# U's first half in a decoder layer: matmuls of 512 columns instead of 256, and an addition of two sums

## The chip, the core and the metric

The kernel runs on one core of one Trainium2 chip. Five engines with queues of their own work on one on-chip memory: TensorE (PE) multiplies matrices into the eight PSUM banks, VectorE (DVE) and ScalarE (ACT) do element-wise work and read PSUM, GpSimd (POOL) does very little here, and SyncE (SP) issues the transfers from HBM. The metric is the device time of one execution, in microseconds (us). Every engine takes its instructions in the order of its queue; where an instruction needs a result of another engine it waits for a semaphore, and all that is queued behind it on its engine waits too.

## The reference

One decoder layer on 256 tokens of 1024 channels. First a mixer (a state-space model and attention, side by side), a residual and a LayerNorm; then PEER, a retrieval over 128 x 128 single-neuron experts, a residual and a second LayerNorm. The change lies in PEER:

```python
q = (xc @ w_q).astype(jnp.float32).reshape(TOKEN_CHUNK, PEER_HEADS, 2, PEER_HALF)
s = jnp.einsum('thcd,hcnd->thcn', q, sub_keys.astype(jnp.float32))
s1, i1 = lax.top_k(s[:, :, 0], PEER_TOPK)
s2, i2 = lax.top_k(s[:, :, 1], PEER_TOPK)
...
top, pos = lax.top_k(cand, PEER_TOPK)
eidx = jnp.take_along_axis(cidx, pos, axis=-1)
g = jax.nn.softmax(top, axis=-1)
u = expert_u[eidx].astype(jnp.float32)
act = jax.nn.gelu(jnp.einsum('td,thkd->thk', xc.astype(jnp.float32), u))
out = jnp.einsum('thk,thkd->td', g * act, expert_v[eidx].astype(jnp.float32))
```

## The kernel before

It gathers no experts. It computes the activation of all 16384 experts for all 256 tokens (x times U), multiplies by gates that are zero for experts not chosen, and multiplies by V. U and V come in 128 tiles each, a tile being 128 experts x 1024 channels in fp32, 512 KB.

*Precision.* A product in full precision is made of three in a faster type (fp32r): each operand is split into an upper half (a rounded copy, `hi`) and a lower half (the rest, `lo`), and hi x hi, hi x lo and lo x hi are summed in PSUM; lo x lo is left out. For U's first half `split3` does this with the weights: ACT casts `hi` (L78), DVE subtracts for `lo` (L79). The transfer's buffer `raw` has four copies, `hi` and `lo` three each. The normed activations stand in x's halves `xh` and `xl`, split once.

*U, a tile.* `dense` (L1122 on) makes 24 matmuls at L1129: for each of 8 slices of 128 channels a weight block of 128x128 is loaded into the array, and 256 columns (the tokens) of x run past it. The order is hi with xh, hi with xl, lo with xh, eight each, all into one sum of 128 experts x 256 tokens.

*U, first half.* Tiles 0 to 63, two at a time in `u_pair` (L854 to L860): both sums lie in one bank of the pool `psb` (two banks), and one ACT instruction takes the gelu from PSUM into the store `act` (L859). Beside it runs the routing, on DVE mostly (`route`: top-16 searches L812 to L816, index arithmetic L879 to L917; `weigh`: the softmax and two groups of transposes on PE, L935). The routing is cut into 44 steps which are handed out over the first 26 pairs, behind each pair's last subtraction. Its index copies `fv` (L908) are on ACT.

*U, second half.* Tiles 64 to 127, again through `dense`; beside them the gates are made (PE L1004, ACT L998, DVE L993 to L995 and L1011), in the pool `pw` (four banks).

*V.* For each tile of V PE makes 12 matmuls of 512 columns (L1056), with blocks of the activations as the weights in the array and the V tile running past.

The order on each engine follows from a scheduler that goes by priorities and data; it is fixed when the kernel is built. In the mixer, two stretches of memory that later hold `xh` and `xl` (tags `xh`, `xl`) hold the transposed input `xT` and a tile of attention weights; at the very end they hold two V tiles.

Of the kernel before, what the change touches and what calls it, by code (L numbers as in the profile page):

```python
# [8 lines left out]
F32 = mybir.dt.float32  # L9
F32R = mybir.dt.float32r  # L10
# [5 lines left out]
OP = mybir.AluOpType  # L16
# [3 lines left out]
D = 1024  # L20
T = 256
ND = D // 128
# [31 lines left out]
def layer(ctx, tc, I, out, tap=None, upto=None):  # L54
    nc = tc.nc
    V, S, P, PE = nc.vector, nc.scalar, nc.gpsimd, nc.tensor

    const = ctx.enter_context(tc.tile_pool(name="const", bufs=1))
# [3 lines left out]
    def load(src):  # L62
        raw = stream.tile([128, 1024], F32, tag="raw", bufs=RAWB, name="raw")
        nc.sync.dma_start(raw, src.rearrange("p a b -> p (a b)") if len(src.shape) == 3 else src)
        return raw

    def split(raw, eng=V, hi=None, lo=None):
        if hi is None:
            hi = stream.tile([128, 1024], F32R, tag="hi", bufs=HIB, name="hi")
            lo = stream.tile([128, 1024], F32R, tag="lo", bufs=LOB, name="lo")  # L70
        S.copy(hi, raw)  # L71
        eng.tensor_tensor(lo, raw, f32(hi), op=OP.subtract)  # L72
        return hi, lo

    def split3(raw):
        hi, lo = (stream.tile([128, 1024], F32R, tag=t, bufs=n, name=t)
                  for t, n in (("hi", HIB), ("lo", LOB)))
        S.copy(hi, raw)  # L78
        return hi, lo, V.tensor_tensor(lo, raw, f32(hi), op=OP.subtract)  # L79
# [20 lines left out]
    def pbank(shape):  # L100
        return ps.tile(shape, F32, tag="w", bufs=4, name="pw")

    def sbank(shape):
        return ps.tile(shape, F32, tag="s", bufs=2, name="psb")

    def abank(shape):
        return ps.tile(shape, F32, tag="a", bufs=2, name="pa")
# [3 lines left out]
    with ExitStack() as px:  # L111
# [6 lines left out]
        with ExitStack() as mx:  # L118
            sb = mx.enter_context(tc.tile_pool(name="sb", bufs=1))
# [5 lines left out]
                return P if CFG[g][i] == "P" else V  # L125

            prm = se.tile([128, 1088], F32, name="prm")
            xT = const.tile([128, ND, T], F32, tag="xh", name="xT")
            nc.sync.dma_start(prm[:, 0:48], I["prm"][:, 0:48])


# [357 lines left out]
            def masks():  # L489
# [5 lines left out]
                for j in range(4):  # L495
# [6 lines left out]
            rs = sb.tile([128, 2, 8], F32, name="rs")  # L502

            pTs = [sb.tile([128, 4, 2, 128], F32, name="pT0"),
                   const.tile([128, 4, 2, T], F32, tag="xl", name="pT1")]

            def attend(b):

# [148 lines left out]
            for k in (4, 5, 6, 7):  # L657
                if k in LATE:
                    r = W3[:, 2 * (k - 6):2 * (k - 6) + 2]
# [7 lines left out]
            for k, t in enumerate(("Kin", "qk")):  # L667
                r = sb.tile([128, 2, 1024], F32R, tag=t, name="W0")
# [8 lines left out]
            ng = sb.tile([128, D], F32, tag="Rt", name="ng")  # L677
            S.activation(ng, g1[:, 0], AF.Copy, scale=-1.0)
            h1b = sb.tile([128, 2, D], F32, tag="rot", name="h1b")
            xh = const.tile([128, ND, T], F32R, tag="xh", name="xh")  # L680
            xl = const.tile([128, ND, T], F32R, tag="xl", name="xl")

            st = {}

# [41 lines left out]
            for q in range(4):  # L726
# [6 lines left out]
                if q < 2:  # L733
                    r = late.tile([128, 2, 1024], F32R, tag="W4", bufs=2, name="W4")
                    hi, lo = r[:, 0], r[:, 1]
                else:
                    hi, lo = (stream.tile([128, 1024], F32R, tag=t, bufs=n, name=t)
                              for t, n in (("hi", HIB), ("lo", LOB)))
# [57 lines left out]
    act = [None, None]  # L796
# [7 lines left out]
    with ExitStack() as rx:  # L804
        sb = rx.enter_context(tc.tile_pool(name="rt", bufs=1))
# [23 lines left out]
        for hc in range(4, 16):  # L829
            raw = load(I["w_q"][hc])  # L830
            if hc == 4:
                with tc.issue_after(w4dma.ins):
                    nc.sync.dma_start(keys, I["keys"])
            hi, lo = (stream.tile([128, 1024], F32R, tag=t, bufs=n, name=t)
                      for t, n in (("hi", HIB), ("lo", LOB)))
# [4 lines left out]
            pt = abank([128, 2, T])[:, 0]  # L840
# [11 lines left out]
            tap("sco", sco)  # L852

        def u_pair(i):  # L854
            pt = sbank([128, 2, T])
            for r in range(2):
                hi, lo, low = split3(load(I["u"][i + r]))
                dense(PE, pt[:, r], hi, lo, xh, xl)
            return low, S.activation(act[0][:, i // 2].rearrange("p t r -> p r t"), pt,  # L859
                                     AF.Gelu_apprx_tanh)  # L860

        gn = sb.tile([128, 2, 128], F32, name="gn")
# [90 lines left out]
        for n in range(HALF // 2):  # L953
            low, ac = u_pair(2 * n)
            with tc.issue_after(low.ins), tc.issue_after(ac.ins) if n >= PAIRS else ExitStack():
                while done < min(STEPS, -(-STEPS * (n + 1) // PAIRS)):
                    done += 1
                    next(steps, None)
                if n == PAIRS - 1:
                    assert next(steps, 0) == 0  # L960
                if n >= PAIRS + GAP - 1:
                    next(last, None)
# [6 lines left out]
    def v_split(half, i, own=None):  # L969
        hi, lo, wh, wl = own or (None, None) + tuple(  # L970
            wk.tile([128, T], F32R, tag=t, bufs=2, name=t) for t in ("wh", "wl"))
        hi, lo = split(load(I["v"][half * HALF + i]), V, hi, lo)
        S.copy(wh, of_tile(half, i))  # L973
        V.tensor_sub(wl, of_tile(half, i), f32(wh))  # L974
        return hi, lo, wh, wl
# [4 lines left out]
    with tc.tile_pool(name="gk", bufs=1) as gk:  # L980
# [41 lines left out]
        for n in range(HALF // 2):  # L1022
# [5 lines left out]
            pt = sbank([128, 2, T])  # L1028
            for r in range(2):
                hi, lo = split(load(I["u"][HALF + 2 * n + r]))  # L1030
# [28 lines left out]
    def v_tile(half, i, t=None):  # L1059
        t = t or v_split(half, i)  # L1060
        for b in range(2):
            v_mm(b, t, half == 0 and i == 0, False)
# [13 lines left out]
    LAST = 4  # L1076
    for i in range(HALF - LAST):
        v_tile(1, i)
    xs = [const.tile([128, 2, 1024], F32R, tag=t, name="vx") for t in ("xh", "xl")]
    last = [v_split(1, HALF - LAST + i, None if i < 2 else  # L1080
                    (xs[0][:, i - 2], xs[1][:, i - 2]) + tuple(
                        wk.tile([128, T], F32R, tag=t, bufs=2, name="wx") for t in ("wx", "wy")))
            for i in range(LAST)]
    st = {}
# [37 lines left out]
def dense(PE, pt, hi, lo, xh, xl, last=None, beside=None):  # L1122

    order = [(hi, xh), (hi, xl), (lo, xh)]
    if last is xl:
        order = [(hi, xh), (lo, xh), (hi, xl)]
    for n, (w, x) in enumerate(order):
        for d in range(ND):
            PE.matmul(pt, w[:, 128 * d:128 * d + 128], x[:, d], start=n == 0 and d == 0,  # L1129
                      stop=n == 2 and d == ND - 1)  # L1130
        if beside is not None and n == 1:
            next(beside, None)
# [76 lines left out]
```

## Time and profile before

| | |
|---|---|
| median of 3 runs | 978.0 us (975.91 to 979.0) |
| the profiled execution | 976.38 us, its span 974.6 us |
| granted TensorE clock, mean | 0.988 |
| PE busy | 953.0 us, 98% |
| DVE busy | 683.7 us, 70% |
| ACT busy | 527.6 us, 54% |
| L1129 (U) and L1056 (V) in the chain that ended last | 38% and 35% |

The page sums busy time over stages with different limits; what the change is worth is read from U's first half alone, which runs from 210 to 396 us. A matmul's record is longer than the distance to the next one, since matmuls are pipelined, so PE's pace is read from the starts in the timeline.

### The profile page before, as it was taken

What the parts mean: (1) busy time and instruction counts of PE and PEld (TensorE: products, weight loads), DVE (VectorE), ACT (ScalarE), POOL (GpSimd) and SP (SyncE); (2) the same over time, 40 slices, a digit from 0 to 9 for tenths busy, and PEclk for the clock granted to TensorE, in tenths of its full rate; (3) what the DMA queues carried; (4) which work ended last, traced back from release to release, by engine and by line L of the source; (5) the groups of instructions that cost most, each with busy time, mean ns of one, the idle gap of its engine ahead of it and who ended that gap; (6) DMA issues with size and microseconds to landing.
All of it is one profiled execution on the core that took longest, in us unless ns stands there. A gap on an engine that the chain in (4) does not pass through costs nothing.

```text
span 974.6 us, 16536 instructions
## 1 busy us (share of the span) xinstructions
PE 953.0 (98%) x6286; PEld 851.0 (87%) x6286; DVE 683.7 (70%) x1431; ACT 527.6 (54%) x995; POOL 21.4 (2%) x25
## 2 busy tenths in 40 slices
PE   7999999999999999999999999999999999999995
PEld 3876977999999999999999999888888888888884
DVE  8974477997777664978889887555555555555556
ACT  3214454555445446888778776455555555555552
POOL 3000002000000000000000000000000000000002
PEclk9996999999999999999999999999999999999998
DMA  8320283356565555455545455556666676666661
GB/s 331 124 66 23 70 274 114 127 186 198 180 187 182 181 187 179 147 156 167 155 140 165 152 153 160 174 192 194 191 196 194 193 278 193 195 194 195 195 194 44
DMA packets 49791, 166.25 MB, mean 171 GB/s; under 512 B 5296, under 2 KB 9392, under 8 KB 49584
## 3 DMA queue, kind: packets, MB, share of 16 engines
q1 hardware_dynamic: 49712, 165.20, 53.6%
q8 instruction: 49, 0.80, 0.3%
q14 instruction: 30, 0.25, 0.1%
HBM read 163.09 MB, written 2.10 MB: 169 GB/s over the span
## 4 chain that ended last, share of the span: by engine, by line
PE 93%; DVE 4%; DMA 1%; ACT 1%; issue 0%; SPq 0%; DVEq 0%; ACTq 0%
PE psb L1129 38%; PE pw L1056 35%; PE pw L1004 3%; PE pw L174 3%; PE pa L1129 2%; PE pw L653 2%; PE psb L163 2%; PE pw L519 1%; PE pa L163 1%; DMA w<-in_w_in 1%; PE pw L394 1%; PE psb L448 1%; PE pa L754 1%; PE pw L544 1%; DMA tail<-in_ln_g 1%; PE pa L533 0%
## 5 line engine op out<-in xcount | busy, mean ns | idle before, releaser
L72 DVE TENSOR_TENSOR lo<-raw,hi 128x1024 fp32r<-128x1024 f32 x195 | 238.6, 1224 | 156.4 <-ACT hi L71 152.3
L71 ACT CAST hi<-raw 128x1024 fp32r<-128x1024 f32 x195 | 205.0, 1051 | 217.2 <-PE pw L1056 162.7
L1056 PE MATMUL pw<-hi,wh 128*128 128x512 f32 x492 | 152.0, 390 | 1.0 <-ACT wh L973 1.0
L1056 PE MATMUL pw<-hi,wl 128*128 128x512 f32 x492 | 152.3, 390 | 0.2
L1056 PE MATMUL pw<-lo,wh 128*128 128x512 f32 x492 | 151.9, 390 | 0.0
L1129 PE MATMUL psb<-xh,lo 128*128 128x256 f32 x1024 | 148.5, 288 | 0.0
L1129 PE MATMUL psb<-xh,hi 128*128 128x256 f32 x1024 | 144.5, 284 | 0.4 <-ACT act L859 0.4
L1129 PE MATMUL psb<-xl,hi 128*128 128x256 f32 x1024 | 143.6, 283 | 0.0
L1129 PEld LDWEIGHTS psb<-xh,hi 128*128 128x128 f32 x1024 | 132.1, 192 | 0.8 <-ACT act L859 0.8
L1129 PEld LDWEIGHTS psb<-xl,hi 128*128 128x128 f32 x1024 | 132.1, 192 | 0.0
L1129 PEld LDWEIGHTS psb<-xh,lo 128*128 128x128 f32 x1024 | 131.2, 192 | 0.0
L78 ACT CAST hi<-raw 128x1024 fp32r<-128x1024 f32 x64 | 67.0, 1047 | 87.4 <-PE psb L1129 78.2
L79 DVE TENSOR_TENSOR lo<-raw,hi 128x1024 fp32r<-128x1024 f32 x64 | 78.1, 1220 | 51.3 <-ACT hi L78 51.1
L1056 PEld LDWEIGHTS pw<-hi,wh 128*128 128x128 f32 x492 | 92.3, 188 | 20.4 <-ACT wh L973 1.4
L1056 PEld LDWEIGHTS pw<-hi,wl 128*128 128x128 f32 x492 | 92.3, 188 | 20.1 <-DVE wl L974 1.1
L1056 PEld LDWEIGHTS pw<-lo,wh 128*128 128x128 f32 x492 | 92.4, 188 | 19.1
L998 ACT ACTIVATE o<-eq,gL 128x128 f16<-128x128 f16 x256 | 85.1, 440 | 0.6 <-DVE eq L994 0.6
L1011 DVE TENSOR_TENSOR act<-pw,act 128x256 f32<-128x256 f32 x124 | 38.3, 351 | 26.6 <-PE pw L1004 26.4
L973 ACT CAST wh<-act 128x256 fp32r<-128x256 f32 x123 | 51.3, 418 | 0.8 <-PE pw L1056 0.8
L974 DVE TENSOR_TENSOR wl<-act,wh 128x256 fp32r<-128x256 f32 x123 | 51.3, 418 | 0.0
L1004 PE MATMUL pw<-o,o 128*128 128x128 f16 x512 | 40.3, 220 | 0.0
L1004 PEld LDWEIGHTS <-o 128*128 128x128 f16 x512 | 29.5, 97 | 2.6
(307 smaller groups left out, 977.4 us busy)
## 6 DMA issues: line engine op xcount, KB each, us to landing
raw<-in_u SPq DMA_DIRECT2D x128, 512.0 KB, 3.5
raw<-in_v SPq DMA_DIRECT2D x128, 512.0 KB, 3.6
w<-in_w_in SPq DMA_DIRECT2D x15, 512.0 KB, 8.5
raw<-in_w_q SPq DMA_DIRECT2D x12, 512.0 KB, 3.8
raw<-in_w_out SPq DMA_DIRECT2D x8, 512.0 KB, 3.9
raw<-in_w_q SPq DMA_DIRECT2D x8, 256.0 KB, 3.9
xT<-in_xT SPq DMA_DIRECT2D x4, 256.0 KB, 5.1
raw<-in_w_glu SPq DMA_DIRECT2D x2, 512.0 KB, 3.7
```

The lines of the kernel that those rows point to most:

```text
L71: S.copy(hi, raw)
L72: eng.tensor_tensor(lo, raw, f32(hi), op=OP.subtract)
L78: S.copy(hi, raw)
L79: return hi, lo, V.tensor_tensor(lo, raw, f32(hi), op=OP.subtract)
L163: PE.matmul(pt[b], xT[:, d, 128 * b:128 * b + 128], w[:, 512 * k:512 * k + 512], start=d == 0, stop=d == 7)
L973: S.copy(wh, of_tile(half, i))
L974: V.tensor_sub(wl, of_tile(half, i), f32(wh))
L998: S.activation(o2[:, 1, i // 2, :, i % 2], eq[:, i // 2, :, i % 2], AF.Copy, scale=gL[:, t0 + i:t0 + i + 1])
L1004: PE.matmul(pt[:, i], o1[:, (q + i) // 2, :, i % 2], o2[:, k, (q + i) // 2, :, i % 2], start=k == 0, stop=k == 1)
L1011: V.tensor_tensor(a, gp[:, :, HALF // 2 * h:HALF // 2 * h + n], a, op=OP.mult)
L1056: PE.matmul(acc[b][c], x[:, tk], w[:, 512 * c:512 * c + 512], start=first and j == 0, stop=last and j == 2)
L1129: PE.matmul(pt, w[:, 128 * d:128 * d + 128], x[:, d], start=n == 0 and d == 0, stop=n == 2 and d == ND - 1)
```

## The change

In U's first half the upper weights meet both halves of x in one matmul of 512 columns. For that `xh` and `xl` become one tile `x2`, in which the 256 columns of xh and the 256 of xl of a channel slice lie side by side. The sum over xh (with the lower weights' products) and the sum over xl now stand beside each other in one bank. ACT copies the second out of PSUM (`ul`), DVE adds it to the first (`us`), and the gelu reads `us`. The sums lie in the four-bank pool `pw` now. One upper slice is left to the end of the tile, behind the lower weights, since it closes the sum over both halves.

```diff
@@ layer: the tiles of x
-            xT = const.tile([128, ND, T], F32, tag="xh", name="xT")
+            x0 = const.tile([128, 2, ND * T], F32, tag="x2", name="x0")
+            xT = x0[:, 0].rearrange("p (d t) -> p d t", t=T)
...
-                   const.tile([128, 4, 2, T], F32, tag="xl", name="pT1")]
+                   x0[:, 1].rearrange("p (n i t) -> p n i t", n=4, i=2)]
...
-            xh = const.tile([128, ND, T], F32R, tag="xh", name="xh")
-            xl = const.tile([128, ND, T], F32R, tag="xl", name="xl")
+            x2 = const.tile([128, ND, 2, T], F32R, tag="x2", name="x2")
+            xh, xl = x2[:, :, 0], x2[:, :, 1]
...
         def u_pair(i):
-            pt = sbank([128, 2, T])
+            us = sb.tile([128, 2, T], F32, tag="us", bufs=2, name="us")
             for r in range(2):
                 hi, lo, low = split3(load(I["u"][i + r]))
-                dense(PE, pt[:, r], hi, lo, xh, xl)
-            return low, S.activation(act[0][:, i // 2].rearrange("p t r -> p r t"), pt,
+                pt = pbank([128, 2, T])
+                for d in range(ND - 1):
+                    PE.matmul(pt, hi[:, 128 * d:128 * d + 128], x2[:, d], start=d == 0, stop=False)
+                for d in range(ND):
+                    PE.matmul(pt[:, 0], lo[:, 128 * d:128 * d + 128], xh[:, d], start=False, stop=False)
+                PE.matmul(pt, hi[:, D - 128:], x2[:, ND - 1], start=False, stop=True)
+                ul = sb.tile([128, T], F32, tag="ul", bufs=2, name="ul")
+                S.copy(ul, pt[:, 1])
+                V.tensor_tensor(us[:, r], pt[:, 0], ul, op=OP.add)
+            return low, S.activation(act[0][:, i // 2].rearrange("p t r -> p r t"), us,
                                      AF.Gelu_apprx_tanh)
```

PE's queue, two tiles of U's first half, before (the tile `psb` is the sum, `hi` and `lo` the weights):

```order
L1129 MATMUL psb<-xh,hi 128x256 x8
L1129 MATMUL psb<-xl,hi 128x256 x8
L1129 MATMUL psb<-xh,lo 128x256 x8
L1129 MATMUL psb<-xh,hi 128x256 x8
L1129 MATMUL psb<-xl,hi 128x256 x8
L1129 MATMUL psb<-xh,lo 128x256 x8
```

and now, where `x_1087` is x2 and `pw` the sum:

```order
L864 MATMUL pw<-x_1087,hi 128x512 x7
L866 MATMUL pw<-x_1087,lo 128x256 x8
L867 MATMUL pw<-x_1087,hi 128x512
L864 MATMUL pw<-x_1087,hi 128x512 x7
L866 MATMUL pw<-x_1087,lo 128x256 x8
L867 MATMUL pw<-x_1087,hi 128x512
```

A tile has 16 matmuls instead of 24, and its last one uses the upper weights.

ACT's queue at the start of U's first half, before (from the score copies of the routing, `sco`, to the third gelu):

```order
L824 COPY sco<-pw 128x128 x5
L78 CAST hi<-raw 128x1024 x2
L859 ACTIVATE act_1317<-psb 128x2x256
L908 CAST fv<-topi 128x2048
L78 CAST hi<-raw 128x1024
L908 CAST fv<-topi 128x2048
L78 CAST hi<-raw 128x1024
L859 ACTIVATE act_1317<-psb 128x2x256
L78 CAST hi<-raw 128x1024 x2
L859 ACTIVATE act_1317<-psb 128x2x256
```

and now:

```order
L826 COPY sco<-pw 128x128 x5
L869 COPY ul<-pw 128x256
L78 CAST hi<-raw 128x1024
L869 COPY ul<-pw 128x256
L78 CAST hi<-raw 128x1024
L871 ACTIVATE act_1315<-us 128x2x256
L920 CAST fv<-topi 128x2048
L869 COPY ul<-pw 128x256
L78 CAST hi<-raw 128x1024
L920 CAST fv<-topi 128x2048
L869 COPY ul<-pw 128x256
L78 CAST hi<-raw 128x1024
```

Each cast `hi`, which is for the tile three ahead, stands behind a copy `ul`, and of the two `fv` one stands ahead of the copy for tile 2 and one ahead of that for tile 3.

DVE's queue, from the subtraction for tile 2 to behind that for tile 3, before:

```order
L79 TENSOR_TENSOR lo<-raw,hi 128x1024
L812 MAX tops<-sco 128x8
L813 MAX_INDEX topi<-tops,sco 128x8
L814 MATCH_REPLACE tmp<-tops,sco 128x128
L815 MAX tops<-tmp 128x8
L816 MAX_INDEX topi<-tops,tmp 128x8
L79 TENSOR_TENSOR lo<-raw,hi 128x1024
L812 MAX tops<-sco 128x8 x2
L813 MAX_INDEX topi<-tops,sco 128x8
```

and now:

```order
L79 TENSOR_TENSOR lo<-raw,hi 128x1024
L814 MAX tops<-sco 128x8
L815 MAX_INDEX topi<-tops,sco 128x8
L816 MATCH_REPLACE tmp<-tops,sco 128x128
L817 MAX tops<-tmp 128x8
L818 MAX_INDEX topi<-tops,tmp 128x8
L870 TENSOR_TENSOR us<-pw,ul 128x256
L79 TENSOR_TENSOR lo<-raw,hi 128x1024
L814 MAX tops<-sco 128x8 x2
L815 MAX_INDEX topi<-tops,sco 128x8
L816 MATCH_REPLACE tmp<-tops,sco 128x128
L870 TENSOR_TENSOR us<-pw,ul 128x256
```

The addition for a tile stands ahead of the subtraction for the tile three ahead; the routing's searches stand behind it.

## Rows read from the trace of the kernel before

**Rows 1.** The page: its head, its first part and its fourth part.

```profile
span 974.6 us, 16536 instructions
PE 953.0 (98%) x6286; PEld 851.0 (87%) x6286; DVE 683.7 (70%) x1431; ACT 527.6 (54%) x995; POOL 21.4 (2%) x25
...
PE 93%; DVE 4%; DMA 1%; ACT 1%; issue 0%; SPq 0%; DVEq 0%; ACTq 0%
PE psb L1129 38%; PE pw L1056 35%; PE pw L1004 3%; PE pw L174 3%; PE pa L1129 2%; PE pw L653 2%; PE psb L163 2%; PE pw L519 1%; PE pa L163 1%; DMA w<-in_w_in 1%; PE pw L394 1%; PE psb L448 1%; PE pa L754 1%; PE pw L544 1%; DMA tail<-in_ln_g 1%; PE pa L533 0%
```

**Rows 2.** The chain in order of time: start us, us, engine, tile, line, count.

```profile
210.96 177.49 PE psb L1129 x1479
388.48 1.05 ACT hi L71
389.53 0.55 ACT act L859
...
624.64 162.11 PE pw L1056 x714
```

**Rows 3.** Five stretches of the span; their columns stand in the first line.

```profile
core 0: us, PE busy (x) PEld busy (x) DVE busy (x) ACT busy (x) POOL busy (x), PEclk, DMA share, GB/s
211.00:349.24 138.24, 138.24 (x1154) 138.24 (x1153) 104.26 (x293) 70.18 (x78) 0.00 (x0) 1.00 0.61 187
349.24:388.48 39.24, 39.24 (x329) 39.24 (x328) 19.40 (x22) 20.35 (x23) 0.00 (x0) 1.00 0.60 188
624.60:786.80 162.20, 162.16 (x715) 134.42 (x716) 93.05 (x121) 80.97 (x118) 0.00 (x0) 1.00 0.61 192
211.00:222.52 11.52, 11.52 (x98) 11.52 (x97) 9.99 (x37) 6.71 (x8) 0.00 (x0) 1.00 0.70 213
222.52:234.04 11.52, 11.52 (x98) 11.52 (x97) 9.64 (x41) 7.02 (x9) 0.00 (x0) 1.00 0.64 204
```

**Rows 4.** Timeline of PE in U's first half: start us, us, engine, line, instruction.

```profile
299.96 1.12 PE L1129 MATMUL psb<-xh,hi 128*128 128x256 f32 x8
...
300.92 1.12 PE L1129 MATMUL psb<-xl,hi 128*128 128x256 f32 x8
...
301.88 1.12 PE L1129 MATMUL psb<-xh,lo 128*128 128x256 f32 x8
```

**Rows 5.** Timeline of PE in V.

```profile
703.20 0.62 PE L1056 MATMUL pw<-hi,wl 128*128 128x512 f32 x2
703.65 0.62 PE L1056 MATMUL pw<-lo,wh 128*128 128x512 f32 x2
704.11 0.62 PE L1056 MATMUL pw<-hi,wh 128*128 128x512 f32 x2
704.56 0.62 PE L1056 MATMUL pw<-hi,wl 128*128 128x512 f32 x2
```

**Rows 6.** Groups of the whole span by shape: count, busy us, mean ns, idle before.

```profile
L843 ACT COPY qT<-pa 128x256 f32<-128x256 f32 x12 | 4.5, 372 | 0.0
...
L1011 DVE TENSOR_TENSOR act<-pw,act 128x256 f32<-128x256 f32 x64 | 27.1, 424 | 26.6 <-PE pw L1004 26.4
...
L917 DVE TENSOR_TENSOR df<-best 128x128 f32<-128x128 f32 x2 | 0.6, 284 | 0.0
```

**Rows 7.** Groups of DVE and ACT from 211 to 388.5 us.

```profile
L79 DVE TENSOR_TENSOR lo<-raw,hi 128x1024 fp32r<-128x1024 f32 x63 | 76.9, 1220 | 51.3 <-ACT hi L78 51.1
...
L78 ACT CAST hi<-raw 128x1024 fp32r<-128x1024 f32 x61 | 63.8, 1046 | 83.6 <-PE psb L1129 78.2 <-DVE abf L896 2.5 <-DVE topi L816 1.8
L859 ACT ACTIVATE act<-psb 128x512 f32<-128x512 f32 x30 | 19.4, 648 | 0.0
```

**Rows 8.** Timeline of ACT at the start of U.

```profile
218.74 1.90 ACT L908 CAST fv<-topi 128x2048 bf16<-128x2048 uint32 x1 [1.45 <-DVE topi L816]
220.54 1.04 ACT L78 CAST hi<-raw 128x1024 fp32r<-128x1024 f32 x1
221.49 1.89 ACT L908 CAST fv<-topi 128x2048 bf16<-128x2048 uint32 x1
```

**Rows 9.** Timeline of PE at the start of U and at the seam.

```profile
209.99 0.36 PE L1129 MATMUL psb<-xh,hi 128*128 128x256 f32 x1
210.25 0.71 PE L823 MATMUL pw<-keys,qT 128*128 128x128 f32 x4
210.72 1.08 PE L1129 MATMUL psb<-xh,hi 128*128 128x256 f32 x7
...
389.46 0.27 PE L935 MATMUL psb<-ident,gn 128*128 128x128 f32 x1
390.12 1.10 PE L1129 MATMUL psb<-xh,hi 128*128 128x256 f32 x7 [0.39 <-ACT act L859]
```

More of the change, by code (lines that the diff above doesn't have):

```diff
@@ L1078, in layer @@
         v_tile(1, i)
-    xs = [const.tile([128, 2, 1024], F32R, tag=t, name="vx") for t in ("xh", "xl")]
+    xs = const.tile([128, 2, 2, 1024], F32R, tag="x2", name="vx")
     last = [v_split(1, HALF - LAST + i, None if i < 2 else
-                    (xs[0][:, i - 2], xs[1][:, i - 2]) + tuple(
+                    (xs[:, 0, i - 2], xs[:, 1, i - 2]) + tuple(
                         wk.tile([128, T], F32R, tag=t, bufs=2, name="wx") for t in ("wx", "wy")))
```

## The prediction

> **What bounds the kernel now.** I read the page first: its first part gives each engine's busy time, its fourth the chain of work that ended last [rows 1]. TensorE (PE) is busy 98% of the span and holds 93% of the chain; two lines carry three quarters of it, L1129 (the U products, 38%) and L1056 (the V products, 35%). The reader is to see that only PE's time counts, unless a change makes another engine late. The chain in order of time [rows 2] then says where PE runs without a pause: in the first half of U for 177.49 us (1479 matmuls in one piece), and in V for 162.11 us. Before the last two tiles of that half is one seam where ScalarE (ACT) is on the chain for 1.6 us. The stretches [rows 3] say the same: in U's first half PE is busy for all of 138.24 us, VectorE (DVE) 104.26 and ACT 70.18, and the granted clock is 1.00 there and in V, so both stretches are at the 2.4 GHz level and their rows may be compared.
>
> PE's busy time says nothing of its pace, since matmuls overlap. The pace is the distance between starts in the timeline. In U eight 256-column matmuls start every 0.96 us [rows 4], 120.0 ns each; 177.49 us over 1479 is the same. In V six 512-column matmuls take from 703.20 to 704.56 us [rows 5], 226.7 ns each (162.11 over 714 gives 227.0). Both have a 128x128 weight load of their own and the same operand type. Twice 120.0 is 240.0: a matmul of double width is 13.3 ns cheaper than two, so each has a fixed part of about 13 ns beside its columns. The whole change lives on that.
>
> **The change part by part.** (a) *Matmuls.* A tile of U had 24 matmuls of 256 columns, 24 x 0.1200 = 2.880 us. Now it has 8 of 512 (upper weights against both halves of x) and 8 of 256 (lower weights): 8 x 0.2267 + 8 x 0.1200 = 2.773 us. That is 0.107 us less in each of 64 tiles, 512 pairs merged: -6.8 us, all on the path. No column is saved. The bounds: if the fixed part goes wholly with the merged weight load, 13.3 ns a pair is what V's rows say; from 227.0 ns it is 13.0, 6.7 us. If a 512-column matmul in this place kept 240 ns, nothing is gained.
>
> The row shows about 13 ns of fixed cost per matmul at the 2.4 GHz level [rows 4, 5]. The Trainium skill (TensorE: Matmul & The Clock Gate, "Back-to-back issue gap") gives the isolated gap as columns over 2.4 plus about 2.5 ns. By it the merge would save 512 x 2.5 ns = 1.3 us, an estimate from that page, and the change would not be seen; the trace disagrees with its 109 ns at 256 columns by 11 ns and with its 216 ns at 512 by the same 11, so here the measurement decides.
>
> (b) *The two sums.* Each tile adds an ACT copy of 128x256 from PSUM and a DVE addition of 128x256 with one operand in PSUM. The copy has a row of exactly its shape, L843 at 372 ns. For the addition the nearest is L1011 at 424 ns (PSUM and SBUF in, strided out); from below, half the elements take 284 ns at L917 [rows 6]. I take 0.424. Over 64 tiles that is 23.8 us of ACT and 27.1 us of DVE. The gelu reads SBUF instead of PSUM; at 648 ns [rows 7] I leave it as it is.
>
> All of it lies beside PE if both engines keep up. ACT: 70.18 us in 48 tiles is 1.46 us a tile (138.24 / 2.880 = 48), 1.83 with the copy, of 2.773. DVE: 104.26 / 48 = 2.17, with the addition 2.60 of 2.773, 94%. In the first eight tiles DVE is denser: 9.99 + 9.64 us [rows 3] are 2.45 a tile, 2.88 with the addition, 0.10 more than PE takes, so it falls 0.8 us behind in eight tiles. From 349 us on (39.24 us, 19.40 of DVE) there is room.
>
> (c) *The wait.* The addition waits for the copy, which waits for the tile's last matmul; behind the addition DVE has the subtraction for the lower weights of the tile three ahead, and behind the copy ACT has that tile's cast (the order shows both). Let a tile end at E. Copy 0.37, cast 1.05, subtraction 1.22 [rows 6, 7] end at about E + 2.7. PE wants those lower weights two tiles and seven 512-column matmuls later, at E + 2 x 2.773 + 7 x 0.227 = E + 7.1. That is 4.4 us of cover. The upper weights are now read to the tile's end and so their buffer comes free a third of a tile later than before; this is inside the same E, since the cast stands behind the copy anyhow. In the trace the cast waits for PE (83.6 us of idle before it, 78.2 of them ended by PE), and the subtraction for the cast (51.1) [rows 7]: both run as soon as a buffer comes free and are far ahead of PE.
>
> The tightest place is where ACT makes two 1.9 us index copies (fv), at 218.74 and 221.49 us [rows 8]. They now stand ahead of the copies and casts of tiles 2 and 3 in ACT's queue. Tile 0 begins at 209.99 and four score matmuls cut in for 0.6 us [rows 9], so tile 6 starts at 210.6 + 6 x 2.773 = 227.2. The first fv waits for an index of DVE, which now has two additions (0.85 us) ahead of it: 219.6. From there ACT does fv, copy, cast, fv, copy, cast: 2 x (1.89 + 0.37 + 1.05) = 6.6 us, so tile 6's upper weights are there at 226.2: 1.0 us to spare. The second such place, near 291 us, is like it with a less loaded DVE. I put +0.3 us for stalls, from 0 to +2.
>
> (d) *PSUM.* The first half's sums leave the two-bank pool for the four-bank pool, so a late addition holds PE only after four tiles. At the seam the transposes of the routing results take one of the two banks, and PE waited for a gelu from 389.57 (389.46 and its 0.11) to 390.12 [rows 9]: 0.55 us that go. What is late there next is the gate products' ACT work, which now begins a little earlier; from 0 to -0.8, I take -0.5.
>
> (e) *Layout.* x's halves lie interleaved in one tile. No instruction outside U's first half changes place apart from the scheduling around the seam, and the second half reads 256 contiguous columns as before. The weights come at 187 GB/s in U's first half [rows 3]; 2.880 / 2.773 of that is 194, and V takes 192 without a pause of PE. Nothing, within +-0.5.
>
> Sum: -6.8 - 0.5 + 0.3 = -7.0 us. The profiled execution took 976.4 us (its span 974.6 and 1.8 around it), so 969.4. The median of the runs is 978.0, 1.6 above it, and the forecast for a median is 978.0 - 7.0 = 971.0.
>
> **The rivals.**
> 1. *DVE and ACT give part of it back.* For it: 94% load in 48 tiles, over 100% in eight, and the fv places. Against: 1.0 us and more of cover at the tightest. If tiles 5 to 8 stall 1 us each, and near 291 us again as much in half, 3 to 4 us return: 974.5.
> 2. *The double width costs 240 ns here*, or the fixed part is as small as a page has it. For it: the operand order differs from V's (weights stationary, x moving, an output that covers a bank of two halves). Against: the widths in [rows 4, 5] share the same surplus. Gain 0 to 1.3 us, with the seam 0.5: 977. The rule is that of the Trainium skill named in (a), as far as the traces bear it out.
> 3. *Slower: DVE becomes the bound by waiting at its addition.* DVE is in order; if it always reaches the addition before ACT's copy is done, it stands for the copy (0.37 and the hand-over, some 0.5 us) with the routing work queued behind, and a tile costs 2.17 + 0.42 + 0.50 = 3.09 us. Over 48 tiles that is 48 x (3.09 - 2.88) = +10.3, less 16 x 0.107 = 1.7 for the others: 978.0 + 8.6 = 986.6. It decides from a wait of 0.28 us a tile on. For it: the addition sits in the order close behind the previous subtraction. Against: a DVE that lags does not wait, one that waits has caught up, and 4.4 us of cover stand between it and PE; it takes a shorter cover than the buffers give.
>
> **How the numbers follow.** The forecast 0.71, rival 1 0.12, rival 2 0.09, rival 3 0.08. A measurement of this kernel can tell about 0.3%, 2.9 us, from no change. The forecast is faster, with little left over; rival 1 mostly (0.08 of 0.12); rival 2 is the same; rival 3 slower, or, where it is mild, the same (0.01). Faster 0.79, same 0.14, slower 0.07. The forecast's own range is -4.5 to -8.5: 969.5 to 973.5. The runs before spread from 975.9 to 979.0, so a median may lie 2 us off; the range takes rivals 1 and 2 in: 968 to 977.5.
>
> **What would show it.** In the profile after: starts of the 512-column matmuls 0.227 us apart, the 256-column ones 0.120, a tile every 2.77 us; U's first half without a pause and about 7 us shorter; DVE some 25 us busier and still waiting for the cast in most tiles from 349 us on; the copy near 0.37 and the addition near 0.42 us; no wait for a gelu at the seam. I am wrong if the starts lie 0.240 apart (rival 2), if the U lines have idle time ended by the cast or the subtraction in many tiles (rivals 1 and 3), or if time is lost in the second half or in V, where I count none.

## The result, and the profile after

The change makes the kernel 0.6% faster: 971.87 us against 978.1 us (medians of five runs each), a ratio of 0.9942 with a 95% interval of 0.9926 to 0.9957. The forecast was 971.0 us.

The profiled execution of the changed kernel took 973.51 us (span 971.7), only 2.9 us less than that of before. That is one execution against one, and its mixer ran at a lower granted clock. The same work up to the output projection's last piece, once at 0.94 and once at 0.91 of full clock (columns as in [rows 3]), before:

```profile
0.00:131.40 131.40, 124.02 (x653) 94.12 (x654) 95.82 (x259) 47.92 (x108) 8.68 (x17) 0.94 0.40 132
```

and after:

```profile
0.00:133.67 133.67, 126.11 (x653) 96.08 (x654) 97.08 (x260) 48.88 (x109) 8.68 (x17) 0.91 0.39 132
```

Each kernel's runs spread over some 4 us by that clock (with this change 969.22 us at a mean of 0.990, 973.51 at 0.984), so I compare stages within the traces, where U and V run at 1.00, beside the medians. The two ends of U are in the chain in order of time: the last piece of the routing's projection and V's first. Before:

```profile
206.47 2.87 PE pa L1129 x24
...
614.18 7.75 PE pw L1056 x34
```

and after:

```profile
208.74 2.87 PE pa L1141 x24
213.24 1.62 PE pw L864 x7
214.86 0.95 PE pw L866 x8
...
610.14 7.75 PE pw L1068 x34
```

From 206.47 to 614.18 are 407.71 us, from 208.74 to 610.14 are 401.40: U's whole stage is 6.3 us shorter, where I had 7.0. The one piece of 1479 matmuls of [rows 2] now shows as groups of 7, 8 and 1, since the width changes.

PE's pace in the timeline after, a tile and its neighbours, to be held against [rows 4] and [rows 5]:

```profile
302.24 0.40 PE L867 MATMUL pw<-x,hi 128*128 128x512 f32 x1
302.47 1.77 PE L864 MATMUL pw<-x,hi 128*128 128x512 f32 x7
304.08 1.12 PE L866 MATMUL pw<-x,lo 128*128 128x256 f32 x8
305.03 0.40 PE L867 MATMUL pw<-x,hi 128*128 128x512 f32 x1
305.27 0.62 PE L864 MATMUL pw<-x,hi 128*128 128x512 f32 x2
```

From 302.47 to 305.27 a tile takes 2.80 us; over many tiles of the chain it is 2.793 (213.24 to 383.64 us in 61 tiles). The eight 256-column matmuls start 0.119 us apart, (305.03 - 304.08) / 8. The eight 512-column ones take 304.08 - 302.24 = 1.84 us, 0.230 each, not 0.2267. Of the terms of (a) it is the one that came out another way.

The stretch with the routing, to be held against the first of [rows 3]:

```profile
212.99:351.00 138.01, 138.01 (x792) 121.41 (x791) 122.13 (x344) 85.89 (x128) 0.00 (x0) 1.00 0.61 191
```

PE is busy for the whole of it; DVE has gone from 104.26 to 122.13 us, ACT from 70.18 to 85.89, and neither holds PE. The groups after, from 212 to 394 us, which answer to [rows 6] and [rows 7]:

```profile
L79 DVE TENSOR_TENSOR lo<-raw,hi 128x1024 fp32r<-128x1024 f32 x64 | 78.0, 1219 | 15.2 <-ACT hi L78 14.5
...
L870 DVE TENSOR_TENSOR us<-pw,ul 128x256 f32<-128x256 f32 x64 | 26.7, 418 | 11.9 <-ACT ul L869 11.1
...
L869 ACT COPY ul<-pw 128x256 f32<-128x256 f32 x64 | 23.8, 371 | 64.4 <-PE pw L867 64.4
L871 ACT ACTIVATE act<-us 128x512 f32<-128x512 f32 x32 | 21.6, 676 | 1.6 <-DVE us L870 1.3
```

The copy and the addition have the durations of the rows chosen for them (371 against 372, 418 against 424 ns). The copy waits for PE 64.4 us in all, so ACT still stands idle in most tiles until PE is done. DVE's idle time ahead of the subtraction fell from 51.3 to 15.2 us; that is DVE's spare time, not yet the cover. The cover, from the end of a tile's subtraction to the first matmul that reads its lower weights, is 4.3 us on the median of the 64 tiles (6.1 before), where (c) had 4.4.

The tightest place, ACT's timeline after, to be held against [rows 8]:

```profile
221.42 1.90 ACT L920 CAST fv<-topi 128x2048 bf16<-128x2048 uint32 x1
...
223.23 0.36 ACT L869 COPY ul<-pw 128x256 f32<-128x256 f32 x1
223.49 1.05 ACT L78 CAST hi<-raw 128x1024 fp32r<-128x1024 f32 x1
...
224.44 1.90 ACT L920 CAST fv<-topi 128x2048 bf16<-128x2048 uint32 x1
...
226.24 0.37 ACT L869 COPY ul<-pw 128x256 f32<-128x256 f32 x1
226.50 1.06 ACT L78 CAST hi<-raw 128x1024 fp32r<-128x1024 f32 x1
```

The last cast is tile 6's and ends at 227.56. PE starts that tile at 229.85:

```profile
229.85 0.86 PE L864 MATMUL pw<-x,hi 128*128 128x512 f32 x3
```

That leaves 2.3 us to spare, the least of all tiles for the upper weights.

### The profile page after: what moved, and what is told of

The parts are those of the page before. It is cut to its first block, busy times and chain, and to the rows that moved or that the text cites. A ratio compares the mean times of both kernels' runs of the same rounds, so it can differ in the third digit from the quotient of the medians.

```text
span 971.7 us, 15703 instructions
## 1 busy us (share of the span) xinstructions
PE 949.5 (98%) x5774; PEld 825.5 (85%) x5774; DVE 705.2 (73%) x1495; ACT 546.6 (56%) x1059; POOL 21.4 (2%) x25
## 4 chain that ended last, share of the span: by engine, by line
PE 93%; DVE 4%; DMA 1%; issue 1%; ACT 0%; SPq 0%; DVEq 0%; ACTq 0%
PE pw L1068 35%; PE psb L1141 19%; PE pw L864 11%; PE pw L866 6%; PE pw L1016 3%; PE pw L175 3%; PE pa L1141 2%; PE pw L654 2%; PE psb L164 2%; PE pw L867 2%; PE pw L520 1%; PE pa L164 1%; PE pw L395 1%; DMA w<-in_w_in 1%; PE psb L449 1%; DMA tail<-in_ln_g 1%
## 5 line engine op out<-in xcount | busy, mean ns | idle before, releaser
L1141 PE MATMUL psb<-x,hi 128*128 128x256 f32 x1024 | 133.3, 283 | 0.0
L1141 PEld LDWEIGHTS psb<-x,hi 128*128 128x128 f32 x1024 | 127.4, 192 | 0.0
L864 PE MATMUL pw<-x,hi 128*128 128x512 f32 x448 | 113.5, 392 | 0.0
L864 PEld LDWEIGHTS pw<-x,hi 128*128 128x128 f32 x448 | 84.2, 188 | 16.4
L79 DVE TENSOR_TENSOR lo<-raw,hi 128x1024 fp32r<-128x1024 f32 x64 | 78.0, 1219 | 15.2 <-ACT hi L78 14.5
L1141 PE MATMUL psb<-x,lo 128*128 128x256 f32 x512 | 76.5, 292 | 0.0
L866 PEld LDWEIGHTS pw<-x,lo 128*128 128x128 f32 x512 | 69.8, 190 | 5.0
L866 PE MATMUL pw<-x,lo 128*128 128x256 f32 x512 | 71.4, 282 | 0.0
L1141 PEld LDWEIGHTS psb<-x,lo 128*128 128x128 f32 x512 | 65.1, 191 | 0.0
L869 ACT COPY ul<-pw 128x256 f32<-128x256 f32 x64 | 23.8, 371 | 64.4 <-PE pw L867 64.4
```

The lines of the kernel that those rows point to most:

```text
L864: PE.matmul(pt, hi[:, 128 * d:128 * d + 128], x2[:, d], start=d == 0, stop=False)
L866: PE.matmul(pt[:, 0], lo[:, 128 * d:128 * d + 128], xh[:, d], start=False, stop=False)
```

## The experiments

In the table the second column is the median, the third the ratio to the runs of before on the same chip with its interval. "U" is the time from the last start of a matmul of the routing's projection to the first start of one of V, and "V" from its first to its last, each from one profile, in us.

| kernel | median | ratio | U | V |
|---|---|---|---|---|
| before | 978.1 | | 404.95 | 350.1 |
| the change | 971.87 | 0.9942 (0.9926 to 0.9957) | 398.64 | 351.2 |
| narrow | 975.57 | 0.9979 (0.9966 to 0.9992) | 404.16 | 349.9 |
| interleave | 973.8 | 0.9954 (0.9939 to 0.9968) | 400.26 | 350.0 |
| nosums | 970.66 | 0.9912 (0.9898 to 0.9927) | 398.65 | 349.8 |
| second | 967.81 | 0.9885 (0.9871 to 0.9899) | 395.18 | 350.1 |
| all512 | 1024.53 (one run) | | 452.03 | 350.0 |
| adds3 | 983.63 | 1.0063 (1.0042 to 1.0085) | 411.70 | 349.8 |
| psb | 973.08 | 0.9944 (0.9925 to 0.9963) | 400.24 | 350.3 |

**narrow**: is it the merging?

```diff
-                for d in range(ND - 1):
-                    PE.matmul(pt, hi[:, 128 * d:128 * d + 128], x2[:, d], start=d == 0, stop=False)
+                for d in range(ND):
+                    PE.matmul(pt[:, 1], hi[:, 128 * d:128 * d + 128], xl[:, d], start=d == 0, stop=d == ND - 1)
+                for d in range(ND - 1):
+                    PE.matmul(pt[:, 0], hi[:, 128 * d:128 * d + 128], xh[:, d], start=d == 0, stop=False)
...
-                PE.matmul(pt, hi[:, D - 128:], x2[:, ND - 1], start=False, stop=True)
+                PE.matmul(pt[:, 0], hi[:, D - 128:], xh[:, ND - 1], start=False, stop=True)
```

> The change with its 512-column matmuls taken apart again: 24 matmuls of 256 columns a tile, while the copy, the addition, the four-bank pool and the joint tile of x stay. If the gain is the merging (512 fewer matmuls with some 13 ns of fixed cost each), a tile costs 2.88 us again, 64 x (2.880 - 2.793) = 5.6 us come back, and the time is about 977.5, with only the half microsecond of the seam left of the gain. If the gain comes from the pool or from the new order of the engines' queues, the time stays near 972.

PE's timeline, a tile:

```profile
303.12 1.12 PE L864 MATMUL pw<-x,hi 128*128 128x256 f32 x8
304.08 1.00 PE L866 MATMUL pw<-x,hi 128*128 128x256 f32 x7
304.92 1.12 PE L868 MATMUL pw<-x,lo 128*128 128x256 f32 x8
305.88 0.28 PE L869 MATMUL pw<-x,hi 128*128 128x256 f32 x1
306.00 0.28 PE L864 MATMUL pw<-x,hi 128*128 128x256 f32 x1
```

2.88 us from 303.12 to 306.00, and U takes 404.16 us: 5.5 us of the 6.3 are back, 0.8 stay with the pool and the seam. Counted from start to start, the U matmuls of the first half take 184.5 us here and 179.0 in the change: the 5.5 us lie in them. The stages say what the first of the two explanations said. The ratio says some 2 us (0.9979) where the stages leave 0.8 (and so do the spans of the two profiled executions, 973.8 against 974.6). Part of that is the clock: 9 of the 17 runs of before on that chip had a mean of 0.985 (978.66 to 979.21 us), 9 of the 12 of this kernel 0.987 or more. At 0.990 the two are level (974.78 against 974.7 and 974.99), at 0.989 this kernel has 974.5 to 975.97 against 976.16 and 976.66, but at 0.987 it has 975.11 to 975.85 against 977.78 to 978.56, so the clock does not account for all of it. So the merging is most of the gain, 4 to 5.5 us of some 6.3, and whether more than 0.8 us is left beside it stays open. A merged pair loses a matmul and a weight load together; which of the two the fixed part belongs to no run separates.

**interleave** and **all512**: where 0.020 us a tile went.

```diff
 interleave
                 for d in range(ND - 1):
                     PE.matmul(pt, hi[:, 128 * d:128 * d + 128], x2[:, d], start=d == 0, stop=False)
-                for d in range(ND):
                     PE.matmul(pt[:, 0], lo[:, 128 * d:128 * d + 128], xh[:, d], start=False, stop=False)
+                PE.matmul(pt[:, 0], lo[:, D - 128:], xh[:, ND - 1], start=False, stop=False)
 all512
-                    PE.matmul(pt[:, 0], lo[:, 128 * d:128 * d + 128], xh[:, d], start=False, stop=False)
+                    PE.matmul(pt, lo[:, 128 * d:128 * d + 128], x2[:, d], start=False, stop=False)
```

> The change with the 512-column and the 256-column matmuls taken in turn, slice by slice, the same 16 matmuls a tile. A tile came out at 2.793 us, 0.020 above 2.773. If the 0.020 are the price of one return from 256 to 512 columns, seven returns a tile cost 0.14 and a tile takes 2.91 us: 64 x 0.12 = 7.7 us more than the change, 979.6. If a 512-column matmul simply takes 229 ns in this place, a tile stays at 2.79 us and the time at 972.

> The lower weights too meet both halves of x: 16 matmuls of 512 columns a tile in U's first half and none of 256 (the products of the two lower halves, which the reference's precision does not ask for, are added). Much slower on purpose: some 64 x 0.85 = 54 us. It is for the pace. If a 512-column matmul is dear (0.233 us) only for the first few behind 256-column ones, here all start 0.227 us apart and a tile takes 16 x 0.2267 = 3.627 us. If it costs 0.230 in this place whatever its neighbours are (x moving, weights stationary, a bank of two sums), a tile takes 3.68 us.

PE's timeline of interleave, in the middle of a tile:

```profile
303.00 0.40 PE L864 MATMUL pw<-x,hi 128*128 128x512 f32 x1
303.23 0.28 PE L865 MATMUL pw<-x,lo 128*128 128x256 f32 x1
303.35 0.40 PE L864 MATMUL pw<-x,hi 128*128 128x512 f32 x1
303.59 0.28 PE L865 MATMUL pw<-x,lo 128*128 128x256 f32 x1
303.71 0.40 PE L864 MATMUL pw<-x,hi 128*128 128x512 f32 x1
```

and of all512, a tile:

```profile
302.63 1.75 PE L864 MATMUL pw<-x,hi 128*128 128x512 f32 x7
304.22 1.98 PE L866 MATMUL pw<-x,lo 128*128 128x512 f32 x8
306.04 0.39 PE L867 MATMUL pw<-x,hi 128*128 128x512 f32 x1
306.26 1.07 PE L864 MATMUL pw<-x,hi 128*128 128x512 f32 x4
```

Without a narrow matmul 16 wide ones take 306.26 - 302.63 = 3.63 us, 0.227 each: the place does not make them dear. In turn with narrow ones a pair takes 0.35 to 0.36 us (303.00, 303.35, 303.71) where 0.2267 + 0.120 would be 0.347, and a tile takes 2.82 us. That is neither number that I expected: not 2.79, and not 2.91 by a price of 0.020 for each return, since seven returns cost some 0.05 together. It fits a surplus of about 6 ns for each pair. In the changed kernel five of the eight wide matmuls carry such a surplus: averaged over the tiles, the five behind the narrow ones take 233, 238, 228, 232 and 231 ns to the next start and the last three 227, and the first narrow one behind them takes 113 ns instead of 120. What in the engine makes it stays open.

**nosums**: do the copy and the addition cost anything?

```diff
-            us = sb.tile([128, 2, T], F32, tag="us", bufs=2, name="us")
...
-                ul = sb.tile([128, T], F32, tag="ul", bufs=2, name="ul")
-                S.copy(ul, pt[:, 1])
-                V.tensor_tensor(us[:, r], pt[:, 0], ul, op=OP.add)
-            return low, S.activation(act[0][:, i // 2].rearrange("p t r -> p r t"), us,
-                                     AF.Gelu_apprx_tanh)
+                ac = S.activation(act[0][:, i // 2].rearrange("p t r -> p r t")[:, r], pt[:, 0],
+                                  AF.Gelu_apprx_tanh)
+            return low, ac
```

> Leaves out the copy and the addition in U's first half, and with them the sum over the lower half of x; the gelu reads the first sum from PSUM, once a tile. If both operations are hidden beside TensorE, the time is that of the change within 1 us (971 to 973). If they cost anything, in waits at the index copies or at the seam, it is 2 us or more below the change, 970 or less.

U takes 398.65 us against 398.64: 128 operations with 50.5 us of busy time are hidden. The median is 1.2 us lower, on another chip and within the spread by clock (0.990: 968.73 against 969.22; 0.986: 971.06 and 971.49 against 971.72 and 971.87). I expected 971 to 973; 970.66 is below that by less than this spread.

**adds3**: where the cover ends. The addition stands three times.

```diff
-                V.tensor_tensor(us[:, r], pt[:, 0], ul, op=OP.add)
+                for _ in range(3):
+                    V.tensor_tensor(us[:, r], pt[:, 0], ul, op=OP.add)
```

> The addition is made three times over in U's first half, with the same result. VectorE spent 2.17 us a tile in the 48 tiles with the routing; an addition added 0.30 us of busy time in the change. With three it is 3.1 us by busy time, 3.4 by the row's 424 ns, over the 2.79 of TensorE. If the cover ends where VectorE's time a tile passes TensorE's, the 48 tiles lose 0.3 to 0.6 us each, 14 to 30 us less the cover of some 4 us: 982 to 998, with TensorE waiting for the subtraction. If the additions are hidden whatever they cost, 972.

The routing's stretch and the longest waits that end at PE in it (PEld is TensorE's weight load; engine, line waited for, us in total, times, longest):

```profile
213.00:352.00 139.00, 134.83 (x743) 112.63 (x742) 134.32 (x411) 81.62 (x118) 0.00 (x0) 1.00 0.53 170
...
PEld pw L866 <- DVE lo L79: 6.9, 14, 1.1
PEld pw L864 <- ACT hi L78: 5.3, 11, 1.0
```

DVE is busy for 134.32 of 139.00 us, and PE waits for its subtraction and, less, for the cast. U grows by 13.1 us; put wholly on the 48 tiles that is 0.27 a tile, 3.06 us each, near 2.17 + 3 x 0.30 = 3.07 by busy time and well under 2.17 + 3 x 0.424 = 3.44. So DVE can become the bound, at three additions and not at one. It does so by its load; rival 3 had it stand at its addition for the copy, and that wait is 6.5 us in all here, less than the 11.1 us of the change.

**psb**: the pool and the seam.

```diff
-                pt = pbank([128, 2, T])
+                pt = sbank([128, 2, T])
```

> The sums of U's first half back in the two-bank pool, one bank a tile, all else as in the change. If the pool matters as I said, the wait of 0.5 us at the seam comes back, and a late addition holds TensorE after two tiles instead of four: some 0.3 us at each of the two places with the index copies. About 973, and in the profile 0.5 to 1.2 us more between U's first tile and its last. If the seam had another cause, nothing changes (972).

PE's timeline at the seam:

```profile
385.86 0.27 PE L947 MATMUL psb<-ident,gn 128*128 128x128 f32 x1
386.84 1.88 PE L864 MATMUL psb<-x,hi 128*128 128x512 f32 x7 [0.71 <-DVE us L870]
```

and in the changed kernel, where the next tile follows at once:

```profile
386.49 0.27 PE L947 MATMUL psb<-ident,gn 128*128 128x128 f32 x1
386.52 1.87 PE L864 MATMUL pw<-x,hi 128*128 128x512 f32 x7
```

U takes 1.6 us more than the change. At the seam 0.87 us are the wait (from 385.86 and its 0.11 to 386.84), now for an addition where [rows 9] show one for a gelu. Some 0.5 us more are two short waits for a late addition at the first pair of index copies (tiles 4 and 5, at 223.1 and 226.3 us); at the second pair, where I expected as much, there is none. A little more in all than expected, by the mechanism expected.

**second**: the same in U's second half, the sum added in place in PSUM.

```diff
...
-                dense(PE, pt[:, r], hi, lo, xh, xl, beside=work)
+                pt = sbank([128, 2, T])
+                for d in range(ND - 1):
+                    PE.matmul(pt, hi[:, 128 * d:128 * d + 128], x2[:, d], start=d == 0, stop=False)
+                next(work, None)
+                for d in range(ND):
+                    PE.matmul(pt[:, 0], lo[:, 128 * d:128 * d + 128], xh[:, d], start=False, stop=False)
+                PE.matmul(pt, hi[:, D - 128:], x2[:, ND - 1], start=False, stop=True)
+                ul = gk.tile([128, T], F32, tag="ul", bufs=1, name="ul")
+                S.copy(ul, pt[:, 1])
+                V.tensor_tensor(pt[:, 0], pt[:, 0], ul, op=OP.add)
...
```

> The change made in U's second half too; the sum is added in place in PSUM and the gelu taken once a tile, for want of memory. If TensorE stays the bound there, 64 x 0.087 = 5.6 us more are gained: 966. VectorE has 182 us of work in these 218 us, and 64 additions of 0.33 to 0.42 us make it 203 to 209 of 212, ScalarE 169 and 64 x 0.45 make 198; so the rival, which I hold for likelier here, is that the waits between them reach TensorE and give the gain back: 971 to 980, with idle time of TensorE ended by the cast, the subtraction or the gate products.

The stretch of U's second half:

```profile
392.80:606.90 214.10, 214.10 (x1540) 180.94 (x1539) 202.47 (x385) 192.33 (x569) 0.00 (x0) 1.00 0.49 157
```

My likelier case was wrong: with DVE at 202.47 and ACT at 192.33 of 214.10 us PE is still busy throughout. It beats both kernels: 967.81 us, 1.15% under before. The half is 217.6 - 214.1 = 3.5 us shorter and not 5.6. Here the gate products, 128 columns wide and in another type, stand among the U products; in PE's timeline seven wide matmuls behind 16 of them take 1.70 us:

```profile
500.40 1.09 PE L1016 MATMUL pw<-o,o 128*128 128x128 f16 x16
501.30 1.86 PE L1047 MATMUL psb<-x,hi 128*128 128x512 f32 x7
503.00 0.62 PE L1050 MATMUL psb<-x,lo 128*128 128x256 f32 x4
```

By the single starts in the trace only the first of the seven is long: it takes 0.31 us to the next start, the other six 0.23 each. A first matmul behind a group of gate products is long in the changed kernel too, 0.20 us where a 256-column one takes 0.120 elsewhere. There the gate products stand in 62 groups, here in 73, and ten of these stand ahead of wide matmuls, where the first takes 0.32 us. Summed over the starts, the gate products and the surplus of the first matmul behind each group cost 1.4 us more than in the changed kernel. That is most of the missing 2.1 us; where the rest lies was not tested.

## Why the prediction was right, point by point

- **(a) The matmuls, -6.8 us.** Right in kind, too large by 1.3 us: 64 x (2.880 - 2.793) = 5.6. I took V's 0.2267 us for a 512-column matmul over to a queue in which widths alternate; there it is 0.230 on the mean. [Rows 5] come from a place with one width only, and all512 shows that the width's neighbours, not the place, make the difference. Narrow shows that most of the gain is the merging.
- **(b) The sums, hidden.** Right (nosums). The durations were right too, but for a nearly full engine the price is the busy time: an addition's record is 0.42 us, and an instruction that does not wait starts 0.33 us after the addition does. DVE's busy time in U grew by 0.34 us for each addition (312.6 to 334.2 us for 64) and by 0.27 for each further one in adds3 (to 369.3 for 128). With 0.424 I put DVE's load at 94%, and 122.13 of 138.01 us are 88%. The gelu from SBUF takes 676 ns instead of 648, hidden as well.
- **(c) The wait, +0.3 us.** Right in kind, too cautious in size. PE did not wait once in U's first half, and 2.3 us were to spare at the tightest place instead of 1.0: the index copies began 8.4 us after tile 0 and not 9.0, and ACT's six operations took 6.1 us (221.42 to 227.56) instead of 6.6, since their records overlap too. The cover of 4.4 us came out at 4.3.
- **(d) The seam, -0.5 us.** Right: 0.8 us of U stay in narrow without the merging, and psb gives 1.6 us back, 0.87 of them at the seam.
- **(e) The layout, nothing.** No cost of it shows. The 1.1 us of V in the change's profile is one late transfer of the last norm's parameters (ACT waited 2.52 us for it, before 1.43); with the same code the other profiles of V take 349.8 to 350.3 us.
- **The sum.** -5.6 - 0.7 = -6.3 in the stage, -6.2 between the medians, against -7.0. The mechanism held; the distance to the median, 0.9 us, is smaller than the fault of (a) because (c) and (d), each off by a little the other way, made up for part of it. The profiled execution was put at 969.4 and took 973.5: 2.3 of these 4.1 us are the mixer at its lower clock, 1.1 are V, 0.7 are U.
- **The rivals.** 1 did not come: no stall. 2 did not come; the fixed part of some 13 ns is there, as narrow (0.120 us) and all512 (0.227 us) show. The small one of the Trainium skill (TensorE: Matmul & The Clock Gate, "Back-to-back issue gap"), 2.5 ns beside the columns for the isolated gap, would have given 1.3 us, an estimate from that page; 5.5 were measured by taking the merge apart. 3 did not come; with three additions DVE became the bound, but by its load and not by the wait that rival 3 describes. (The product in rival 3, 48 x (3.09 - 2.88), is 10.1 and not 10.3, which changes nothing.)

## What to carry to other kernels

Where PE is the bound and reloads its weights for every matmul, two narrow matmuls with the same weights are worth merging into a wide one even if no column is saved, as long as the engines that repair the sum have room: here it was worth some 11 ns for each pair (5.5 us over 512). Read the pace from starts in a stretch that has the same neighbours, not only the same shape, and price added work on a nearly full engine by the distance from its start to the next start, not by the duration of one record. And when a gain is a few parts in a thousand, compare stages of the traces at one clock beside the medians.

## What the runs showed of the hardware

A 512-column matmul in this operand type starts 0.227 us after the one before where all are of 512 columns (V, and all512), and on the mean 0.228 to 0.238 us where 256-column ones stand close before it (the change, interleave). A 256-column one takes 0.120 us among its like and 0.113 to 0.119 close behind a wide one. Behind a group of 128-column products in f16 the first matmul of this type takes some 0.08 us longer to the next start (0.20 us at 256 columns), for a wide one 0.09 (0.32 us, second), while the last product of the group is up to 0.03 us shorter. A DVE addition of 128x256 with one operand in PSUM has a record of 418 ns, and the next instruction that does not wait starts 0.33 us after it.
